# A hybrid decoder step on one Trainium2 core: a triangular product cut into two column tiles, transpositions for diagonal products, earlier cached keys, and other ranks

## The chip, the core and the metric

The kernel runs on one core of a Trainium2 chip. TensorE (PE in the profile; its weight loads are listed apart as PEld) multiplies, VectorE (DVE), ScalarE (ACT) and GpSimd (POOL) work on data in SBUF and PSUM, and SyncE (SP) issues the DMAs. Each engine runs its own instructions in order and waits on semaphores for the others. The metric is the device time of one execution in microseconds; lower is better.

## The reference

One inference step of a two-layer trunk with model width 1024, for a prompt of 1024 tokens and for 8 samples of 4 tokens each. Each layer adds a gated branch to its input. Layer 0 is sliding-window attention (16 heads of 64, 4 key and value heads, window 128, one learned sink per head); the samples attend to 128 cached tokens as well. Layer 1 is gated DeltaNet (16 value heads and 8 query and key heads of 128). Cut to what matters here:

```python
def modulate(x, c, norm_g, w_mod, b_mod):
    shift, scale, gate = jnp.split(jax.nn.silu(c) @ w_mod + b_mod, 3, axis=-1)
    return rms_norm(x, norm_g) * (1 + scale[:, None]) + shift[:, None], gate[:, None]

def swa_branch(h, w_in, sinks, w_out, k_buf=None, v_buf=None):
    q, k, v, z = jnp.split(h @ w_in, ..., axis=-1)
    attn = sink_softmax(...) @ v          # over the window, and the cache for samples
    return (attn * jax.nn.silu(z)) @ w_out, new_k, new_v

def gated_delta_chunked(q, k, v, g, beta, s0, chunk):
    ...
    lower = jnp.where(strict, jnp.einsum('nbhik,nbhjk->nbhij', kb, kc) * decay, 0.0)
    rhs = jnp.concatenate([vc * bc[..., None], kb * jnp.exp(gc)[..., None]], axis=-1)
    sol = lax.linalg.triangular_solve(lower + jnp.eye(chunk), rhs, left_side=True, lower=True, unit_diagonal=True)
    ...
    s_final, o = lax.scan(step, s0, (w_v, w_k, qk, q_dec, k_dec, g_tot))

for layer in range(2):
    hp, gp = modulate(xp, c_prompt, ...)          # the same for the samples
    op, *new = swa_branch(...) if layer == 0 else gdn_branch(...)
    xp = xp + gp * op
y_prompt = rms_norm(xp, final_norm_g)
```

## The kernel before

All tensors are float32. A large product (input and output weights of both layers) is made of three float32r products per tile: each operand is split in a high and a low part (`wh`, `wl` for weights, `h2hi`, `h2lo` for activations, `whi`, `wlo` and `ohi`, `olo` for the attention's output weights and their input), and high by high, high by low and low by high are summed in PSUM. These **weight products** (`ps_pj`, and `ps_mi` for the attention's output) are most of TensorE's stream, and they are written out as one long sequence.

Everything else is written as Python generators that `weave` puts in the list `jobs`, sorted by a rank from the tables K, KT (near the end) and KR (one row for each pair of heads). After each weight product `stages()` goes through the list in this order and lets each generator run on as long as the condition that it yields is true. `ready`, `soon` and `idle` compare the time at which a tile is finished, by the estimate of a planner (`Core`), with the time that TensorE has come to; `bank` waits for a PSUM bank, `later`, `pos` and `ticks` count products. So ranks and the other number tables (SP, AT, EX, TB, SW, MS, MM) decide between which weight products a generator's instructions stand in each engine's fixed order. Nearly every instruction is issued through one helper, so its line in the profile is 84.

The places that the change touches:

- `invert`, once for each of eight pairs of heads. It inverts unit lower triangular matrices of 128 rows in blocks of 32: DVE inverts the 32x32 diagonal blocks, POOL writes them transposed and spread into the two tiles `Xd`, and `diagonal()` multiplies, for each of four tiles of four matrices (`UZ`, one tile for a `cp_`), the matrix with `Xd` on TensorE: four products of 128 rows and 128 columns of weights with 96 moving columns. ACT copies the result with its sign turned into `M` (three buffers from the pool). `blocks()` then works the off-diagonal blocks out with narrow products of `M` and `UZ`, 32 columns of weights at a time, in the trace `ps_lg<-UZ,M`.
- `shape(i, ...)`, once for each of nine row blocks of the input of layer 1. It scales the block's rows with the reciprocal root of their mean square and turns the block. Up to step five (i below 5) DVE scales the rows (`xn`) and TensorE transposes four 128x128 pieces for each of two halves; from i = 5 on DVE makes a diagonal matrix `dg` of the scales, and TensorE multiplies the unscaled rows `xt` by it, which turns and scales at once.
- `cached`, once the prompt's attention is finished. It opens a pool, fetches the samples' mask `smk`, and starts four generators `cached_pair`, of two samples each. Each fetches its cached keys `KT` and values `vc` (two buffers of each), then multiplies queries (`qz`) with the cached keys and the new ones (`kxs`).
- `load_wo`, which fetches the attention's output weights in pieces of 128x512 and splits them. Each piece is two DMAs of 64 rows, from two heads' rows.

The lines of `diagonal` that matter most:

```python
for q in range(4):
    nc.tensor.matmul(pmv[:, q, 0:96], uz[:, q, :], xd[:, q, 0:96], start=True, stop=True)
yield soon(pm)
M = gs.tile([P, 4, 96], F32, tag="M", name="M", bufs=3)
nc.scalar.activation(M, pmv[:, :, 0:96], AF.Copy, scale=-1.0)
```

Of the kernel before, what the change touches and what calls it, by code (L numbers as in the profile page):

```python
# [5 lines left out]
F32 = mybir.dt.float32  # L6
# [8 lines left out]
P = 128  # L15
# [282 lines left out]
def body(tc, I, O, cst_ap, dbg=None):  # L298
    nc = tc.nc
# [15 lines left out]

    nkeep = COFF["wmask"][0]
    ZB, VB, SB = 2, 3, 6
    SP = (5, 21)
    AM = (7, 12)
    AT = (-1, 10)  # L320
    EX = (2.2, 1.5, 0.8, 0)
    ES, EN, EL, EM = EX
    K = {'split': 52, 'add': 3, 'attend': 12, 'turning': 14, 'modulate': 16, 'cached': 29, 'wo': 6, 'turn': 0, 'ahead': 2, 'taps': 2, 'gating': 5, 'decay': 27, 'samples': 9, 'load': 6, 'mod': 9, 'shape': 3, 'decays': 33, 'prepare': 1, 'gather': 11, 'finish': 37, 'states': 27, 'core': 2, 'new': 18}
    KT = {'prepare': 0, 'gather': 35, 'finish': 60, 'states': 19, 'core': 7, 'new': 19, 'load': 27, 'gating': 6, 'samples': 7, 'output': 23}
    KR = [{'chain': 1, 'output': 3, 'solve': 5, 'invert': 21, 'blocks': 35, 'decayed': 0}, {'chain': 10, 'output': 4, 'solve': 19, 'invert': 10, 'blocks': 35, 'decayed': 37}, {'chain': 23, 'output': 2, 'solve': 17, 'invert': 19, 'blocks': 33, 'decayed': 9}, {'chain': 23, 'output': 23, 'solve': 3, 'invert': 4, 'blocks': 24, 'decayed': 17}, {'chain': 13, 'output': 3, 'solve': 12, 'invert': 10, 'blocks': 35, 'decayed': 40}, {'chain': 9, 'output': 13, 'solve': 6, 'invert': 20, 'blocks': 51, 'decayed': 28}, {'chain': 0, 'output': 1, 'solve': 16, 'invert': 20, 'blocks': 45, 'decayed': 11}, {'chain': 10, 'output': 6, 'solve': 4, 'invert': 28, 'blocks': 1, 'decayed': 44}]
    TB = (3, 1)
    SW = (1, 10)
    MS = (44, 11)
    AH, AI = (a / 10 for a in AM)
    VK = (1,)  # L330
    MM = (1, 7)
    ORDER = [("q", 2), ("q", 3), ("q", 4), ("q", 5), ("z", 0), ("k", 1), ("z", 1), ("z", 2), ("q", 6), ("q", 7),
             ("z", 3), ("z", 4), ("z", 5), ("z", 6), ("z", 7)]
    SE = ("vector", "vector", "vector", "vector")
# [240 lines left out]
    def ready(*ts):  # L575
        return lambda: plain() or nc.ready(ts) <= nc.free["tensor"]
# [433 lines left out]
    if True:  # L1010
# [271 lines left out]
        def cached():  # L1282

            nonlocal sa_guard, sa
            yield lambda: attended[0] == 4 * NB
            at_guard.__exit__(None, None, None)
            open_wo(4)
            sa_guard = tc.tile_pool(name="sa", bufs=1, side="left")
            sa = Watched(nc, sa_guard.__enter__(), since=nc.free["tensor"])
            smk = sa.tile([P, 4, P + TS], F32, name="smk")  # L1290
            o, w = COFF["smask"]
            nc.sync.dma_start(smk.rearrange("p a c -> p (a c)"), cst_ap[:, o:o + w])
            osb = yield from bank("ob")
# [21 lines left out]
        def cached_pair(b2, smk, osv):  # L1315

            vc_rows = I["cache_swa_v"][0].rearrange("b s h d -> b s (h d)")
            yield lambda: paired[0] >= b2 - 1
# [4 lines left out]
            nc.sync.dma_start(vc, vc_rows[bs].rearrange("b s c -> s b c"))  # L1323
            yield ready(KT)
            lg = yield from bank("lg")
            for c0, c1 in ((P, P + TS), (0, P)):
# [80 lines left out]
        wo_rows = I["swa_w_out"][0]  # L1407
        wo_guards, whi, wlo = [], [], []

        def open_wo(n):  # L1410
# [8 lines left out]
        def load_wo(j0):  # L1419

            pieces = [(j, hf) for j in range(j0, j0 + 4) for hf in range(2)]
            raws_ = []
            if j0:
                yield over("ahead")

            def fetch():
                if pieces:
                    j, hf = pieces.pop(0)
                    pr, g = j // 4, j % 4
# [112 lines left out]
    if True:  # L1542
# [63 lines left out]
        def shape(i, t, xt, ss, parts):  # L1606
# [6 lines left out]
            nc.vector.tensor_scalar(sv, sv, 1.0 / D, EPS, ALU.mult, ALU.add)  # L1613
            rs = sm.tile([P, 1], F32, tag="rs", name="rs")[0:parts]
            rsqrt(nc, sm, rs, sv, 1, parts)
            if i >= 5:
                dg = x2.tile([P, 512], F32, tag="xn", name="dg", bufs=2)[0:parts, 0:parts]
                nc.vector.tensor_scalar_mul(dg, ident[0:parts, 0:parts], rs)
            for kk in range(2):
                if i < 5:  # L1620
                    xn = x2.tile([P, 512], F32, tag="xn", name="xn", bufs=2)[0:parts]
                    yield idle("vector", rs, xt)
                    nc.vector.tensor_scalar_mul(xn, xt[:, kk * 512:(kk + 1) * 512], rs)
                    yield ready(xn)
                else:
                    yield ready(dg, xt)
                pt = yield from bank("lg")
                for q in range(4):
                    if i < 5:
# [102 lines left out]
    gbs = gk.tile([P, 2, HV], F32, name="gbs")  # L1732
    gbT = gk.tile([2 * HV, TS], F32, name="gbT")

    gs, Xd, gs_guard = None, [], None

    def decays():

# [138 lines left out]
    if True:  # L1877
# [205 lines left out]
        def invert(hq, st, Ld, Xdd):  # L2083
# [31 lines left out]
            def diagonal():  # L2115

                for cp_, uz in enumerate(uzs):
# [824 lines left out]
    for b in range(LB + 1):  # L2942
# [14 lines left out]


_INS = ["x_prompt", "x_sample", "cache_swa_k", "cache_swa_v", "state_gdn_s",
        "w_mod", "b_mod", "swa_sinks", "swa_w_out", "gdn_a_log",  # L2960
        "gdn_dt_bias", "gdn_o_norm_g", "gdn_w_out", "final_norm_g"]


def relaid(inputs):
# [18 lines left out]
    more = dict(keep=keep.reshape(2, P, 16, 24),  # L2983
                keysT=A["cache_swa_k"][0].reshape(4, 2, P, 4, 64).transpose(0, 4, 1, 3, 2).reshape(4, 64, 1024),
                sinks_r=np.repeat(np.stack([A["swa_sinks"][0].reshape(4, 4)] * 2, axis=1).reshape(32), 4).reshape(P, 1),
                taps=A["gdn_conv_w"].reshape(P, P).T, gwab=gw[:, :, 6144:6176],
# [35 lines left out]
```

## Time and profile before

| | before |
|---|---|
| median of 3 runs | 1624.63 us |
| the runs | 1621.93 to 1625.57 us |
| the profiled execution | 1620.58 us |
| its span, first to last instruction | 1618.8 us |
| mean granted TensorE clock | 0.994 |
| memory traffic over the span | 121 GB/s |

The profile is of one execution. An engine's busy time counts the time in which at least one of its instructions runs, and each record of a product lasts from its start to its modelled end, so successive records overlap; what a product costs is read from the distance of starts, not from the lengths. A float32 product leaves two records and a float32r product one. In a row such as `ps_lg<-Xd,UZ 128*128 128x96 f32 x8` stand what is written, what is read, the rows and columns of the array in use, the shape of the result, the type and the number of records. A row of waits names who waited for whom. The granted clock is the share of full speed that the throttle leaves TensorE.

### The profile page before, as it was taken

To read this page: it belongs to the slowest core of one execution; us is meant where nothing else is said; L and a number is where in the kernel's file an instruction comes from. 1 tells how busy PE (TensorE), PEld (TensorE's weight loads), DVE (VectorE), ACT (ScalarE), POOL (GpSimd) and SP (SyncE) were. 2 spreads that over 40 slices of the span, in tenths; PEclk is the share of its full clock that TensorE was granted. 3 is DMA by queue.
4 is the path that set the end of the run, shared out by engine and by line. 5 is a ranking of instruction groups with operands and counts; after the bars stand their busy time and mean duration, and the time that the engine had idled before them with its cause. 6 is when DMAs were issued, how large, how long until landed. Compare 5 with 4: busy or idle time off the path is not lost. (4 is left out here: it accounts for less than half of the span.)

```text
span 1618.8 us, 30542 instructions
## 1 busy us (share of the span) xinstructions
PE 1579.1 (98%) x10586; PEld 1403.9 (87%) x10586; DVE 1208.0 (75%) x3773; ACT 841.4 (52%) x2422; POOL 222.4 (14%) x292
## 2 busy tenths in 40 slices
PE   9999999999999999999999999999999999999997
PEld 6888898988778999999989999899999997757776
DVE  5737677565566778977888778887797987848676
ACT  4625555553344646466564664664657564524332
POOL 1300000002222002010020100101002004233433
PEclk9999999999999999999999999999999999999999
DMA  9443200125343333312432324224233236685874
GB/s 363 153 165 105 79 29 28 34 69 135 106 146 108 94 83 85 107 52 77 129 78 80 103 62 121 74 70 115 75 101 91 48 94 200 204 267 182 302 262 159
DMA packets 178827, 195.71 MB, mean 121 GB/s; under 512 B 76848, under 2 KB 120720, under 8 KB 178640
## 3 DMA queue, kind: packets, MB, share of 16 engines
q1 hardware_dynamic: 178672, 193.75, 39.7%
q8 instruction: 84, 1.38, 0.4%
q14 instruction: 71, 0.58, 0.1%
HBM read 146.45 MB, written 49.27 MB: 121 GB/s over the span
## 5 line engine op out<-in xcount | busy, mean ns | idle before, releaser
L84 PE MATMUL ps_pj<-h2hi,wl 128*128 128x384 f32 (+1 forms) x1128 | 379.7, 337 | 2.4 <-DVE wl L84 2.4
L84 PE MATMUL ps_pj<-h2lo,wh 128*128 128x384 f32 (+1 forms) x1128 | 378.1, 335 | 0.0
L84 PE MATMUL ps_pj<-h2hi,wh 128*128 128x384 f32 (+1 forms) x1128 | 378.0, 335 | 0.0
L84 PEld LDWEIGHTS ps_pj<-h2hi,wl 128*128 128x128 f32 x1128 | 212.6, 188 | 6.3 <-DVE wl L84 3.4
L84 PEld LDWEIGHTS ps_pj<-h2hi,wh 128*128 128x128 f32 x1128 | 212.7, 189 | 3.1 <-ACT XR L84 0.5
L84 PEld LDWEIGHTS ps_pj<-h2lo,wh 128*128 128x128 f32 x1128 | 212.8, 189 | 2.6
L84 PE MATMUL ps_pj<-hlo,wh 128*128 128x384 f32 (+1 forms) x376 | 125.1, 336 | 0.1
L84 PE MATMUL ps_pj<-hhi,wh 128*128 128x384 f32 (+1 forms) x376 | 124.2, 332 | 0.7 <-ACT hhi L84 0.4
L84 PE MATMUL ps_pj<-hhi,wl 128*128 128x384 f32 (+1 forms) x376 | 123.5, 332 | 0.0
L84 POOL TENSOR_TENSOR Xd<-Xc,cst 32x128 f32<-32x128 f32 x128 | 66.1, 516 | 414.7 <-DMA Xc<-Xdd 97.5
L84 DVE SCALAR_TENSOR_TENSOR vT<-XR,cT,vT 128x384 f32<-128x384 f32 (+1 forms) x144 | 81.4, 575 | 26.1 <-ACT vT L84 24.7
L84 DVE TENSOR_TENSOR wl<-wr,wh 128x512 fp32r<-128x512 f32 x120 | 82.5, 688 | 11.2 <-ACT wh L84 10.6
L84 POOL TENSOR_TENSOR xt<-xt,y 128x512 f32<-128x512 f32 (+1 forms) x47 | 64.4, 1373 | 164.6 <-DVE y L84 146.6
L84 ACT CAST wh<-wr 128x512 fp32r<-128x512 f32 x128 | 78.5, 615 | 14.3 <-PE ps_pj L84 11.8
L84 PEld LDWEIGHTS ps_pj<-hlo,wh 128*128 128x128 f32 x376 | 71.3, 190 | 11.8 <-issue 10.9
L84 PEld LDWEIGHTS ps_pj<-hhi,wh 128*128 128x128 f32 x376 | 71.3, 190 | 5.4 <-issue 2.7
L84 PEld LDWEIGHTS ps_pj<-hhi,wl 128*128 128x128 f32 x376 | 71.4, 190 | 4.8 <-issue 4.6
L84 ACT ACTIVATE qe<-ps_mi,Eg 128x128 f32<-128x128 f32 x112 | 35.0, 363 | 74.3 <-PE ps_mi L84 74.2
L84 ACT COPY XR<-ps_pj 128x384 f32<-128x384 f32 (+1 forms) x96 | 43.3, 452 | 52.5 <-PE ps_pj L84 52.2
L84 ACT ACTIVATE prob<-prob,nm 128x256 f32<-128x256 f32 (+1 forms) x128 | 62.4, 490 | 15.6 <-DVE nm L84 15.5
L84 DVE TENSOR_TENSOR X<-X,tmp 128x126 f32<-128x126 f32 (+22 forms) x248 | 63.7, 257 | 8.5
L84 DVE TENSOR_TENSOR tmp<-X 128x126 f32<-128x126 f32 (+22 forms) x248 | 62.3, 251 | 7.5 <-POOL X L84 3.2
(557 smaller groups left out, 3861.1 us busy)
## 6 DMA issues: line engine op xcount, KB each, us to landing
wr<-in_gwb SPq DMA_DIRECT2D x96, 256.0 KB
S<-in_states SPq DMA_DIRECT2D x42, 256.0 KB
wm<-in_wm SPq DMA_DIRECT2D x16, 512.0 KB
wr<-in_winb SPq DMA_DIRECT2D x32, 256.0 KB
wmod<-in_w_mod SPq DMA_DIRECT2D x32, 256.0 KB
wm<-in_w_mod SPq DMA_DIRECT2D x32, 256.0 KB
DP<-gcr SPq DMA_DIRECT2D x64, 128.0 KB
zl<-zd SPq DMA_DIRECT2D x32, 256.0 KB
```

What stands on the lines that cost most here:

```text
L84: inst = fn(*args, **kwargs)
```

## The change

The product with `Xd` is cut in two for each matrix, by columns of weights: columns 64 to 127 with 96 moving columns, and columns 32 to 63 with 32. Columns 0 to 31 are no longer computed, and of columns 32 to 63 only the first 32 results. The copy to `M` becomes two operations, and the three buffers of `M` are tiles of their own whose rows 0 to 63 are set to zero once, on POOL.

`shape` scales and transposes in all nine steps (the threshold becomes DG = 9, so `dg` is not made). The cached keys and values of the first two pairs of samples are fetched as soon as the pool is open, ahead of the mask. The host lays the attention's output weights out by pieces (`wob`), and each piece is one DMA of 128 rows. The number tables are others.

```diff
-    SP = (5, 21)
+    SP = (1, 18)
-    AT = (-1, 10)
-    EX = (2.2, 1.5, 0.8, 0)
+    AT = (-1, 13)
+    EX = (1.7, 0.7, 1.0, 0)
-    K = {'split': 52, ... 'modulate': 16, ... 'gather': 11, 'finish': 37, 'states': 27, 'core': 2, 'new': 18}
+    K = {'split': 7, ... 'modulate': 22, ... 'gather': 14, 'finish': 1, 'states': 32, 'core': 0, 'new': 13}
...
-    TB = (3, 1)
-    SW = (1, 10)
-    MS = (44, 11)
+    TB = (3, 0)
+    SW = (2, 24)
+    MS = (60, 4)
-    MM = (1, 7)
+    DG = 9
+    MM = (6, 9)
...
+            held = [cached_rows(b2) for b2 in range(2)]
             smk = sa.tile([P, 4, P + TS], F32, name="smk")
...
-                weave(cached_pair(b2, smk, osv), "cached")
+                weave(cached_pair(b2, smk, osv, held), "cached")
...
+        def cached_pair(b2, smk, osv, held):
+            yield lambda: paired[0] >= b2 - 1
+            KT, vc = held[b2] if b2 < 2 else cached_rows(b2)
             yield ready(KT)
...
-                    for a in range(2):
-                        hd = (2 * pr + a) * 4 + g
-                        nc.sync.dma_start(raw[64 * a:64 * a + 64], wo_rows[hd * 64:hd * 64 + 64, hf * 512:(hf + 1) * 512])
+                    nc.sync.dma_start(raw, I["wob"][j, hf])
...
-            if i >= 5:
+            if i >= DG:
                 dg = x2.tile([P, 512], F32, tag="xn", name="dg", bufs=2)[0:parts, 0:parts]
...
-                if i < 5:
+                if i < DG:
                     xn = x2.tile([P, 512], F32, tag="xn", name="xn", bufs=2)[0:parts]
...
+        for i in range(3):
+            Mx.append(gs.tile([P, 4, 96], F32, name=f"M{i}"))
+            nc.gpsimd.memset(Mx[i][0:64], 0.0)
...
                     for q in range(4):
-                        nc.tensor.matmul(pmv[:, q, 0:96], uz[:, q, :], xd[:, q, 0:96], start=True, stop=True)
+                        for r0, n in ((64, 96), (32, 32)):
+                            rs = slice(r0, 2 * r0)
+                            nc.tensor.matmul(pmv[rs, q, 0:n], uz[:, q, rs], xd[:, q, 0:n], start=True, stop=True,
+                                             skip_group_check=True)
                     yield soon(pm)
-                    M = gs.tile([P, 4, 96], F32, tag="M", name="M", bufs=3)
-                    nc.scalar.activation(M, pmv[:, :, 0:96], AF.Copy, scale=-1.0)
+                    M = Mx[(4 * hq + cp_) % 3]
+                    nc.scalar.activation(M[64:P], pmv[64:P, :, 0:96], AF.Copy, scale=-1.0)
+                    nc.scalar.activation(M[32:64, :, 0:32], pmv[32:64, :, 0:32], AF.Copy, scale=-1.0)
```

In TensorE's order, the first block of products with `Xd` in the program stands like this before; a row gives the line, the operation, what is written and read, and the rows and columns of the result (with the number of products, where several alike follow each other):

```order
L84 MATMUL ps_pj<-h2hi,wl 128x384
L84 MATMUL ps_pj<-h2hi,wh 128x288
L84 MATMUL ps_pj<-h2lo,wh 128x288
L84 MATMUL ps_lg<-Xd_6467,UZ 128x96 x4
L84 MATMUL ps_pj<-h2hi,wl 128x288
```

And like this after, at the same block, between weight products of another width:

```order
L84 MATMUL ps_lg<-erl,qT 128x128 x4
L84 MATMUL ps_pj<-h2hi,wl 128x384
L84 MATMUL ps_lg<-Xd_6488,UZ 64x96
L84 MATMUL ps_lg<-Xd_6488,UZ 32x32
L84 MATMUL ps_lg<-Xd_6488,UZ 64x96
L84 MATMUL ps_lg<-Xd_6488,UZ 32x32
L84 MATMUL ps_lg<-Xd_6488,UZ 64x96
L84 MATMUL ps_lg<-Xd_6488,UZ 32x32
L84 MATMUL ps_lg<-Xd_6488,UZ 64x96
L84 MATMUL ps_lg<-Xd_6488,UZ 32x32
L84 MATMUL ps_pj<-h2hi,wh 128x384
```

Four products in a row have become eight, and the part of the array changes between each and the next. The block stands 111 rows later in the list; what surrounds it is the same kind of weight product.

On SP, at the place where the prompt's attention is finished and `cached` begins, before (`wr` and `wor` are pieces of the attention's output weights, `smk` is the mask, `KT` and `vc` the cached keys and values):

```order
L84 DMA wr<-in_swa_w_out 64x512 x2
L84 DMA smk<-in_cst 128x640
L84 DMA wor<-in_swa_w_out 64x512 x6
L84 DMA KT<-in_keysT 64x1024
L84 DMA vc<-in_cache_swa_v 128x2x256
L84 DMA KT<-in_keysT 64x1024
L84 DMA vc<-in_cache_swa_v 128x2x256
L84 DMA wor<-in_swa_w_out 64x512 x10
```

And after:

```order
L84 DMA wr<-in_wob 128x512 x3
L84 DMA KT<-in_keysT 64x1024
L84 DMA vc<-in_cache_swa_v 128x2x256
L84 DMA KT<-in_keysT 64x1024
L84 DMA vc<-in_cache_swa_v 128x2x256
L84 DMA smk<-in_cst 128x640
L84 DMA wor<-in_wob 128x512 x4
L84 DMA KT<-in_keysT 64x1024
```

The keys have moved ahead of the mask and of the first pieces of weights. On TensorE, 42 weight products stand between the last attention product of the prompt and the first product with keys of the samples before, and 17 after.

On TensorE again, at the first half of step six of `shape`, before (`dg` by the rows `xt`):

```order
L84 MATMUL ps_mi<-whi,ohi 128x512
L84 MATMUL ps_mi<-whi,olo 128x512
L84 MATMUL ps_lg<-dg,xt 128x128 x4
L84 MATMUL ps_mi<-wlo,ohi 128x512
L84 MATMUL ps_mi<-whi,ohi 128x512
```

And after (`xn` are the scaled rows, `erl` the tile with the identity matrix):

```order
L84 MATMUL ps_mi<-whi,olo 128x512
L84 MATMUL ps_mi<-wlo,ohi 128x512
L84 MATMUL ps_lg<-erl,xn 128x128 x4
L84 MATMUL ps_mi<-whi,ohi 128x512
L84 MATMUL ps_mi<-whi,olo 128x512
```

Four products with a diagonal have become four transpositions, and they stand behind a weight product of another part (`wlo,ohi`).

More of the change, by code (lines that the diff above doesn't have):

```diff
@@ L317, in body @@
     ZB, VB, SB = 2, 3, 6
-    SP = (5, 21)
+    SP = (1, 18)
     AM = (7, 12)
-    AT = (-1, 10)
-    EX = (2.2, 1.5, 0.8, 0)
+    AT = (-1, 13)
+    EX = (1.7, 0.7, 1.0, 0)
     ES, EN, EL, EM = EX
-    K = {'split': 52, 'add': 3, 'attend': 12, 'turning': 14, 'modulate': 16, 'cached': 29, 'wo': 6, 'turn': 0, 'ahead': 2, 'taps': 2, 'gating': 5, 'decay': 27, 'samples': 9, 'load': 6, 'mod': 9, 'shape': 3, 'decays': 33, 'prepare': 1, 'gather': 11, 'finish': 37, 'states': 27, 'core': 2, 'new': 18}
@@ L324, in body @@
-    KT = {'prepare': 0, 'gather': 35, 'finish': 60, 'states': 19, 'core': 7, 'new': 19, 'load': 27, 'gating': 6, 'samples': 7, 'output': 23}
-    KR = [{'chain': 1, 'output': 3, 'solve': 5, 'invert': 21, 'blocks': 35, 'decayed': 0}, {'chain': 10, 'output': 4, 'solve': 19, 'invert': 10, 'blocks': 35, 'decayed': 37}, {'chain': 23, 'output': 2, 'solve': 17, 'invert': 19, 'blocks': 33, 'decayed': 9}, {'chain': 23, 'output': 23, 'solve': 3, 'invert': 4, 'blocks': 24, 'decayed': 17}, {'chain': 13, 'output': 3, 'solve': 12, 'invert': 10, 'blocks': 35, 'decayed': 40}, {'chain': 9, 'output': 13, 'solve': 6, 'invert': 20, 'blocks': 51, 'decayed': 28}, {'chain': 0, 'output': 1, 'solve': 16, 'invert': 20, 'blocks': 45, 'decayed': 11}, {'chain': 10, 'output': 6, 'solve': 4, 'invert': 28, 'blocks': 1, 'decayed': 44}]
@@ L326, in body @@
-    TB = (3, 1)
-    SW = (1, 10)
-    MS = (44, 11)
+    K = {'split': 7, 'add': 3, 'attend': 12, 'turning': 14, 'modulate': 22, 'cached': 29, 'wo': 6, 'turn': 0, 'ahead': 2, 'taps': 2, 'gating': 5, 'decay': 27, 'samples': 9, 'load': 6, 'mod': 9, 'shape': 3, 'decays': 33, 'prepare': 1, 'gather': 14, 'finish': 1, 'states': 32, 'core': 0, 'new': 13}
+    KT = {'prepare': 0, 'gather': 15, 'finish': 33, 'states': 19, 'core': 7, 'new': 20, 'load': 37, 'gating': 6, 'samples': 7, 'output': 23}
+    KR = [{'chain': 1, 'output': 3, 'solve': 18, 'invert': 21, 'blocks': 35, 'decayed': 0}, {'chain': 8, 'output': 4, 'solve': 14, 'invert': 10, 'blocks': 35, 'decayed': 37}, {'chain': 23, 'output': 5, 'solve': 17, 'invert': 22, 'blocks': 23, 'decayed': 9}, {'chain': 23, 'output': 23, 'solve': 3, 'invert': 4, 'blocks': 24, 'decayed': 17}, {'chain': 27, 'output': 3, 'solve': 16, 'invert': 10, 'blocks': 35, 'decayed': 38}, {'chain': 9, 'output': 13, 'solve': 6, 'invert': 20, 'blocks': 47, 'decayed': 28}, {'chain': 0, 'output': 1, 'solve': 17, 'invert': 21, 'blocks': 45, 'decayed': 11}, {'chain': 10, 'output': 6, 'solve': 4, 'invert': 12, 'blocks': 1, 'decayed': 44}]
@@ L1313, in body, with cached_rows @@
         paired, looked = [0], [0]
-        def cached_pair(b2, smk, osv):
+        def cached_rows(b2):
             vc_rows = I["cache_swa_v"][0].rearrange("b s h d -> b s (h d)")
-            yield lambda: paired[0] >= b2 - 1
             bs = slice(2 * b2, 2 * b2 + 2)
@@ L1628, in shape @@
                 for q in range(4):
-                    if i < 5:
+                    if i < DG:
                         nc.tensor.transpose(pt[:, q * parts:(q + 1) * parts], xn[:, q * P:(q + 1) * P],
@@ L1733, in body @@
     gbT = gk.tile([2 * HV, TS], F32, name="gbT")
-    gs, Xd, gs_guard = None, [], None
+    gs, Xd, Mx, gs_guard = None, [], [], None
     def decays():
@@ L2959 @@
 _INS = ["x_prompt", "x_sample", "cache_swa_k", "cache_swa_v", "state_gdn_s",
-        "w_mod", "b_mod", "swa_sinks", "swa_w_out", "gdn_a_log",
+        "w_mod", "b_mod", "swa_sinks", "gdn_a_log",
         "gdn_dt_bias", "gdn_o_norm_g", "gdn_w_out", "final_norm_g"]
@@ L2982, in relaid @@
     gw = A["gdn_w_in"][0].reshape(KD, P, -1).transpose(1, 0, 2)
-    more = dict(keep=keep.reshape(2, P, 16, 24),
+    wo = np.asarray(inputs["swa_w_out"])[0].reshape(2, 2, 4, 64, 2, 512).transpose(0, 2, 4, 1, 3, 5)
+    more = dict(wob=wo.reshape(8, 2, P, 512), keep=keep.reshape(2, P, 16, 24),
                 keysT=A["cache_swa_k"][0].reshape(4, 2, P, 4, 64).transpose(0, 4, 1, 3, 2).reshape(4, 64, 1024),
```

3 lines of the change are left out of this document (1 added, 2 removed).

## The prediction

> **What bounds the kernel now.** First the page's header and its busy shares, then the waits of PE, then the timeline of PE around the places that the change touches.
>
> ```profile
> span 1618.8 us, 30542 instructions
> ```
>
> ```profile
> PE 1579.1 (98%) x10586; PEld 1403.9 (87%) x10586; DVE 1208.0 (75%) x3773; ACT 841.4 (52%) x2422; POOL 222.4 (14%) x292
> ```
>
> PE is busy for 98% of the span; the next engine, DVE, for 75%. So 39.7 us are left in which PE is idle, the start and the end of the program among them. Its waits (us in total, times, the longest):
>
> ```profile
> PE ps_mi L84 <- DVE us L84: 4.1, 4, 2.0
> ```
>
> ```profile
> PE ps_lg L84 <- DVE xn L84: 0.2, 1, 0.2
> ```
>
> These are the largest of 26 rows, 30 us together, and one of the smallest (one wait for a scaled block, of which more below), spread from the start to the last output blocks. Nothing waits long. What the kernel takes is therefore the length of PE's own stream: a product that takes longer there lengthens the run by as much, and an operation on another engine costs nothing until PE waits for it. The profiled execution took 1620.58 us, 1.8 more than its span; the three runs have their median 4.1 above it, at 1624.63, and all three lie 1.3 to 5.0 above it.
>
> **Xd's products, the term that decides.** Each of the 32 blocks (eight pairs of heads, four tiles each) has four products on PE, each of which leaves two records, and before they stand between weight products. First a place with a smaller block, for the step between two weight products, then a block of Xd (the columns are start, length to the end of the last, engine, what; 128*128 is rows and columns of the array in use):
>
> ```profile
> 636.68 0.34 PE L84 MATMUL ps_pj<-h2hi,wh 128*128 128x384 f32 x1
> 636.86 0.34 PE L84 MATMUL ps_pj<-h2lo,wh 128*128 128x384 f32 x1
> 637.13 0.44 PE L84 MATMUL ps_lg<-UZ,M 128*32 128x32 f32 x8
> 637.50 0.44 PE L84 MATMUL ps_pj<-h2hi,wl 128*128 128x384 f32 x1
> 637.78 0.34 PE L84 MATMUL ps_pj<-h2hi,wh 128*128 128x384 f32 x1
> ```
>
> ```profile
> 635.09 0.34 PE L84 MATMUL ps_pj<-h2hi,wl 128*128 128x384 f32 x1
> 635.27 1.03 PE L84 MATMUL ps_lg<-Xd,UZ 128*128 128x96 f32 x8
> 636.08 0.42 PE L84 MATMUL ps_pj<-h2hi,wh 128*128 128x384 f32 x1
> 636.34 0.34 PE L84 MATMUL ps_pj<-h2lo,wh 128*128 128x384 f32 x1
> ```
>
> From one weight product to the next is a step of 0.18 (636.68 to 636.86). In the second fence 1.25 us pass from the weight product before the block to the second one after it; without the block they would be two such steps, rather 0.17 than 0.18. The block costs **0.91 us**: eight records of 0.11, and nothing for going in and out.
>
> After, each product becomes two, one into columns 64 to 127 of the array with 96 moving columns and one into columns 32 to 63 with 32. The trace of before has no such pair, but it has narrow products, 128*32, of both widths of movement, 32 columns at 637.13 above and 96 here:
>
> ```profile
> 848.75 0.34 PE L84 MATMUL ps_pj<-h2lo,wh 128*128 128x384 f32 x1
> 849.02 0.85 PE L84 MATMUL ps_lg<-UZ,M 128*32 128x96 f32 x8
> 849.80 0.44 PE L84 MATMUL ps_pj<-h2hi,wl 128*128 128x384 f32 x1
> 850.08 0.34 PE L84 MATMUL ps_pj<-h2hi,wh 128*128 128x384 f32 x1
> ```
>
> By the same reckoning the block of 96 costs 1.33 - 0.34 = 0.99 and that of 32 costs 0.92 - 0.34 = 0.58. The 64 columns between them cost 0.41 over eight records, 0.05 each; in proportion a record of 96 columns is 0.077 and one of 32 is 0.026. That leaves 0.37 in both blocks for going into a narrow part of the array and out again. So a narrow block is no gain by itself even if its two halves run side by side: 0.99 for 0.91.
>
> The question is what it costs to go from a 64-column part to a 32-column part and back, which the new stream does seven times within each block. There is one place before where the two follow each other between products of one size:
>
> ```profile
> 414.29 0.39 PE L84 MATMUL ps_pj<-wlo,ohi 128*64 128x512 f32 x1
> 414.52 0.40 PE L84 MATMUL ps_pj<-whi,ohi 128*64 128x512 f32 x1
> 414.85 1.05 PE L84 MATMUL ps_lg<-modG,sels 128*32 128x512 f32 x2
> 415.83 0.45 PE L84 MATMUL ps_pj<-wlo,ohi 128*64 128x512 f32 x1
> ```
>
> Between two of 128*64 the step is 0.23; to the first of 128*32 it is 0.33, 0.10 more. On the way back two records of 512 columns, 0.41 each at the rate above, fill 0.98: 0.16 more. The weights tell the same:
>
> ```profile
> 414.85 0.14 PEld L84 LDWEIGHTS ps_lg<-modG,sels 128*32 128x32 f32 x2 [0.42 <-issue]
> ```
>
> They are loaded only when their product starts, after 0.42 of idle, and no engine is named that they waited for. And it isn't shared columns that hold them: here the part changes from columns 64 to 127 to columns 0 to 31,
>
> ```profile
> 378.66 0.41 PE L84 MATMUL ps_ob<-spT,vc 128*64 128x16 f32 x6
> 379.00 0.33 PE L84 MATMUL ps_lg<-kxs,qz 64*32 64x32 f32 x16
> ```
>
> and 0.34 pass for six records of 16 columns, which at the 0.03 to 0.04 that they take one after another are 0.2; some 0.13 is left over. So I take it that each change of size empties the array. Then nothing runs side by side: 8 x 0.077 + 8 x 0.026 + 0.37 + seven changes. At 0.10 each the block is 1.89, at 0.16 it is 2.31. If each change cost half of the 0.37, it were 2.49; if none cost anything, and the halves overlapped, 0.99. I take 0.14 between the two directions of the nearest row, 2.17, less the 0.37 where a block follows another narrow one (8 of the 32 by the order of the instructions, so 0.1 on average): 2.07, **1.16 more than before, 37 us for 32 blocks**. The ends are +31 and +51 with emptying, and +2.6 without it.
>
> The Trainium skill has rules for both, in "TensorEngine Tiling (Array Packing)", Tiling Modes, Key Properties: a change of tiling mode, not just of tile, drains TensorE, and it lists 128 x 64 and 128 x 32 as different modes. By that rule the sum is the one with emptying, and the 0.10 at 414.85 agrees with it; no trace of before shows the two sizes side by side on different columns with all 128 rows.
>
> **Steps turned by transposition (DG 5 to 9).** Four blocks, steps six to nine, lose eight groups of four products with a diagonal and get eight groups of four transpositions:
>
> ```profile
> 478.41 0.39 PE L84 MATMUL ps_mi<-whi,olo 128*128 128x512 f32 x1
> 478.64 1.05 PE L84 MATMUL ps_lg<-dg,xt 128*128 128x128 f32 x8
> 479.45 0.48 PE L84 MATMUL ps_mi<-wlo,ohi 128*128 128x512 f32 x1
> 479.76 0.40 PE L84 MATMUL ps_mi<-whi,ohi 128*128 128x512 f32 x1
> ```
>
> ```profile
> 452.96 0.39 PE L84 MATMUL ps_mi<-whi,ohi 128*128 128x512 f32 x1
> 453.19 0.60 PE L84 MATMUL ps_lg<-erl,xn 128*128 128x128 f32 x4
> 453.55 0.48 PE L84 MATMUL ps_mi<-whi,olo 128*128 128x512 f32 x1
> 453.86 0.39 PE L84 MATMUL ps_mi<-wlo,ohi 128*128 128x512 f32 x1
> ```
>
> Less two steps of 0.23, 0.89 becomes 0.44: **-3.6 us**. DVE scales two halves of a row block in place of one diagonal; the earlier steps do that now, and PE waited for xn once, for 0.2, so I take 0; if each of the eight new ones cost as much it were 1.6.
>
> **Cached keys first.** Before, the mask and six half rows of weights stand ahead of the keys on SP's queue, and PE waits:
>
> ```profile
> 354.21 0.33 SPq L84 DMA_DIRECT2D smk<-in_cst  x1
> 354.60 4.53 SPq L84 DMA_DIRECT2D wor<-in_swa_w_out  x6
> 359.18 0.59 SPq L84 DMA_DIRECT2D KT<-in_keysT  x1
> ```
>
> ```profile
> 363.43 0.64 PE L84 MATMUL ps_lg<-KT,qz 64*32 64x128 f32 x16 [2.48 <-DMA vc<-in_cache_swa_v]
> ```
>
> ```profile
> 364.00:368.00 4.00, 4.00 (x45) 3.14 (x42) 1.30 (x8) 0.62 (x1) 0.00 (x0) 0.56 1.06 254
> 368.00:372.00 4.00, 4.00 (x16) 4.00 (x15) 2.28 (x4) 3.04 (x10) 2.32 (x2) 0.59 0.60 143
> ```
>
> The third number from the end of such a window's row is the granted clock: 0.56 and 0.59 of full speed right behind the wait, 1.8 + 1.6 = 3.4 us lost. The wait costs 5.9 in all. After, the keys go out 4.97 earlier against the pool's opening (354.21 in place of 359.18) and took at most 4.3 to land; the order puts their first product 17 weight products behind the last attention block in place of 42, 25 x 0.17 = 4.3 us sooner. So the keys gain about 0.7 us on PE, and more, since 256 KB of keys no longer share the engines with a mask and six loads ahead of them. I take **-4**; the ends are 0 (they still come late) and -5.9. Whole rows of weights halve SP's issues for them; no row of the waits names wor, so 0.
>
> **The eviction in two.** ACT's copy of the product becomes two:
>
> ```profile
> L84 ACT ACTIVATE M<-ps_lg 128x384 f32<-128x384 f32 x32 | 15.7, 489 | 33.2 <-PE ps_lg L84 33.2
> ```
>
> The first of them reads as many columns as that row's, the second a third, so 0.49 is the most that the second can take: 32 x 0.49 = 16 us of ACT, which is 52% busy. What waits for M comes up to 0.49 later in each block; PE has weight products of 0.17 ready in between, three of them, so I take 0 of it; with that cover gone it were 16. Clearing three M tiles on POOL (14% busy) happens once: 0.
>
> **The other ranks and numbers.** They move products on PE among the weight products; neither the count nor the kinds change. What they can give is a part of the 30 us of waits, what they can take are new ones of the same sizes; I take 0 and 8 us either way.
>
> **Sum.** 1620.6 + 37 - 3.6 - 4 = 1650.0. The runs stand 1.3 to 5.0 above the profiled execution; I leave the forecast at **1650**, its own range being 1638 to 1664.
>
> **Rivals.** The first one leans on a place where three narrow tiles stand together:
>
> ```profile
> 840.71 0.85 PE L84 MATMUL ps_lg<-UZ,M 128*32 128x96 f32 x24
> ```
>
> *The halves run side by side.* If a change between parts with different columns empties nothing, a block is 0.99: 2.6 - 3.6 - 4 = -5.0, or 1615.6, and with up to 8 us from the ranks 1609 to 1622. This ends on the other side. For it speaks that 128*32 parts of different columns do run so (24 records in this row last 0.85, as long as the 8 at 849.02); it decides if a change costs under 0.02, since 7 x 32 x 0.02 = 4.5 uses up the gain. Against it stand the three rows above. The Trainium skill says in the same place that different tiles can load weights and multiply in parallel; by that sentence the time would be this rival's. Chance 0.31, of which 0.26 faster and 0.05 within 0.2%. *Emptying at a lower price.* Where only part of the 0.10 is paid (0.04 a change), a block is 1.35 to 1.45: 32 x 0.5 = 16, so 1629. Chance 0.08, slower. *New waits.* The scaled halves, the second eviction or the new order make PE wait 8 to 12 us more, beside either case: 1624 to 1628 with the halves side by side. Chance 0.05, of which 0.02 slower and 0.03 within 0.2%. The forecast has the other 0.56.
>
> Over 0.2%, 3.2 us, is about what a measurement of this kernel can tell from no change. So slower 0.56 + 0.08 + 0.02 = 0.66, within 0.2% 0.05 + 0.03 = 0.08, faster 0.26. Cases of both signs hold the chance, so the range goes from 1610, which takes in most of the first rival, to 1663.
>
> **What would show it.** In the profile after, the four products of a block follow each other at 0.4 to 0.5 us a pair, with their weight loads not ahead of them; PE's busy time rises while its instructions gain only 224 records. A pair every 0.16 shows the rival. The wait for the keys and the clock behind it in the slice at 360 us are gone or not; transpositions of 0.44 stand in steps six to nine. Wrong would the forecast be by the price of a change of size, before all else.

## The result, and the profile after

The changed kernel takes **1663.13 us** (median of 4 runs, 1661.94 to 1664.1) against 1623.28 us before in the same comparison (4 runs): ratio 1.0245, 95% interval 1.0227 to 1.0263. It is slower, as forecast, but by 40 us in place of 25, and it lies just above the range that ended at 1663 (the forecast's own range, before the rivals were joined to it, went to 1664).

The header and the busy shares of the profile after:

```profile
span 1660.2 us, 31020 instructions
PE 1617.9 (97%) x10810; PEld 1410.7 (85%) x10810; DVE 1206.5 (73%) x3777; ACT 854.6 (51%) x2454; POOL 219.6 (13%) x295
```

The span is 41.4 us longer. PE is busy for 38.8 us more with 224 records more (10586 to 10810), and idle for 2.6 us more. So most of the time went into TensorE's stream itself. The timeline of TensorE around the first block with `Xd` (start, length to the end of the last, what) shows where:

```profile
638.09 0.42 PE L84 MATMUL ps_pj<-h2hi,wl 128*128 128x384 f32 x1
638.44 2.02 PE L84 MATMUL ps_lg<-Xd,UZ 128*64 128x96 f32 x16
640.39 0.44 PE L84 MATMUL ps_pj<-h2hi,wh 128*128 128x384 f32 x1
640.66 0.34 PE L84 MATMUL ps_pj<-h2lo,wh 128*128 128x384 f32 x1
```

By the prediction's reckoning the block is 2.57 - 0.35 = 2.22 us (the group's name shows the first of its two forms). Before it was 0.91. The weight loads don't run ahead of the products, as the prediction said of emptying; the first starts only when its product does:

```profile
638.43 1.91 PEld L84 LDWEIGHTS ps_lg<-Xd,UZ 128*64 128x64 f32 x16 [0.18 <-issue]
```

Of the other two terms the profile after shows both effects where they were looked for. The keys land nearly in time, and the clock behind them is full (third number from the end of the window's row):

```profile
363.87 0.64 PE L84 MATMUL ps_lg<-KT,qz 64*32 64x128 f32 x16 [0.57 <-DMA KT<-in_keysT]
```

```profile
364.00:368.00 4.00, 4.00 (x63) 3.35 (x59) 0.74 (x5) 0.19 (x1) 0.00 (x0) 1.00 1.03 334
```

And all nine steps are transposed, with hardly a wait. The row has the eight steps of 128 rows (records, busy time and mean, and the idle time ahead of them); the ninth, of 32 rows, has 8 records of its own:

```profile
L84 PE MATMUL ps_lg<-erl,xn 128*128 128x128 f32 x64 | 9.7, 273 | 0.7 <-DVE xn L84 0.7
```

What was not expected are the first three rows of TensorE's waits:

```profile
PE ps_mi L84 <- DVE us L84: 7.4, 7, 1.6
PE ps_mi L84 <- DVE S L84: 5.4, 7, 1.9
PE ps_mi L84 <- ACT kb L84: 4.8, 5, 1.6
```

They were 4.1, 0.5 and 0.6 before. `us` and `S` belong to the recurrence of layer 1, `kb` to the samples' state updates near the end. They take the place of the keys' wait and of others that are gone.

### The profile page after: what moved, and what is told of

It reads as the page before. It is cut to its first block, busy times and chain, and to the rows that moved or that the text cites. A ratio compares the mean times of both kernels' runs of the same rounds, so it can differ in the third digit from the quotient of the medians.

```text
span 1660.2 us, 31020 instructions
## 1 busy us (share of the span) xinstructions
PE 1617.9 (97%) x10810; PEld 1410.7 (85%) x10810; DVE 1206.5 (73%) x3777; ACT 854.6 (51%) x2454; POOL 219.6 (13%) x295
## 5 line engine op out<-in xcount | busy, mean ns | idle before, releaser
L84 ACT CAST wh<-wr 128x512 fp32r<-128x512 f32 x128 | 78.3, 614 | 28.7 <-PE ps_pj L84 27.6
L84 ACT COPY XR<-ps_pj 128x384 f32<-128x384 f32 (+1 forms) x96 | 43.3, 451 | 45.3 <-PE ps_pj L84 44.7
L84 PE MATMUL ps_lg<-Xd,UZ 128*64 128x96 f32 (+1 forms) x512 | 64.6, 239 | 0.2 <-POOL Xd L84 0.2
```

Of the source, the lines that this page charges most:

```text
L84: inst = fn(*args, **kwargs)
```

## The experiments

**A measure used below.** Where two traces differ in many places, the time from the start of each of TensorE's records to the start of the next is compared with the usual step of its kind (the 30th percentile, over the traces of all kernels here, of steps with the same part of the array, the same width and the same kind of neighbours). The sum of the usual steps is what the stream costs undisturbed; the rest is **delay**, by waits and by a lower clock. Both are worked out from single profiled executions, and over the first 1200 weight products, where nothing is changed but a number or two, kernels differ by up to 1.4 us in it. Against the kernel before, over the whole program:

| kernel | undisturbed stream | delay |
|---|---|---|
| changed kernel | +31.6 | +9.8 |
| before, split products, order kept (o_before_split) | +35.2 | +1.7 |
| changed kernel, whole products, order kept (o_whole) | -3.6 | +16.5 |
| before, DG = 9, order kept (o_dg) | -3.5 | +6.8 |
| before, keys first and whole rows, order kept (o_keys_wob) | 0.0 | +1.7 |

The measure does not serve where two products run side by side, as with even tiles (below): there the starts of two streams lie between each other, 0.01 and 0.08 us apart in turn, and a usual step means little. Where the order is kept, the 32 blocks can be compared directly, from the weight product before a block to the second one after it. Read so, they take 35.5 us more in o_before_split and 0.4 more in o_before_even than in the kernel before, and 36.0 less in o_whole, 35.8 less in o_even and 24.1 less in o_grouped than in the changed kernel.

### One edit undone or done, planned anew

```diff
# e1_xd_only: the kernel before with
+ for r0, n in ((64, 96), (32, 32)): matmul(pmv[rs, q, 0:n], uz[:, q, rs], xd[:, q, 0:n])   # and M in two
# e2_no_xd: the changed kernel with
+ matmul(pmv[:, q, 0:96], uz[:, q, :], xd[:, q, 0:96])                                      # and M in one
# e3_even: the changed kernel with
+ for rs, n in ((slice(64, P), 96), (slice(0, 64), 32)):
# e4_grouped: the changed kernel with the loop over tiles outside the loop over q
```

> The kernel before with one edit, the product with Xd in two column tiles (64 and 32 columns) and M in two evictions; ranks, numbers, DG and DMAs are those of before. If each change of size empties the array, a block costs 2.2 us in place of 0.90 and the kernel takes 32 x 1.2 to 1.3, that is 38 to 42 us more than before: ratio 1.023 to 1.026. If the other ranks and numbers of the changed kernel are what lengthened it, this edit alone gives less than 15 us: ratio under 1.009.

Measured 1682.14 us, ratio 1.0366 (1.0351 to 1.0382): more than the whole change, and more than either theory gave.

> The changed kernel with the product with Xd whole again (128 columns, one eviction of M); ranks, DG = 9, early keys and whole rows of weights stay. If the size changes are the cause, 38 to 42 us go: 1621 to 1625, ratio to before 0.998 to 1.001, and what is left of the difference is what the rest of the change does. If the ranks are the cause it stays above 1645, ratio over 1.013.

Measured 1654.77 us, ratio 1.0201 (1.0182 to 1.0219). Taken alone this would speak for the ranks and against the price of the size changes.

> The changed kernel with the second tile made as wide as the first: columns 0 to 63 with 32 moving columns in place of columns 32 to 63 (the results for columns 0 to 31 are not used). As many products, on different columns, but all of one size. If changes of size are paid, none is left inside a block: 16 records take about 8 x 0.08 and what of 8 x 0.05 does not lie beside them, with 0.37 for entry and exit, so 1.0 to 1.4 a block, 27 to 39 us less than the changed kernel: 1624 to 1636, ratio to before 1.000 to 1.008. If eight narrow products are dear by themselves, whatever their sizes, it stays at 1655 to 1665, ratio over 1.019.

Measured 1640.34 us, ratio 1.0109 (1.0092 to 1.0125).

> The changed kernel with the four products of 64 columns first and then the four of 32: the same products, one change of size inside a block in place of seven. At 0.14 a change a block is 0.84 less: 27 us off the changed kernel, 1636, ratio to before 1.006 to 1.010. If the products are dear by themselves it stays at 1655 to 1665.

Measured 1645.26 us, ratio 1.0128 (1.0101 to 1.0154).

These four don't add up: 58 us for the split put into the one kernel, 8 us for taking it out of the other. The edits are not alone in these runs, because of the planner. It holds an estimate for each product, and a block of other products shifts all later estimates, so that every condition after the first block fires at another place. Each of the four is a new order, and their delay shows it: +29.0 for e1_xd_only and +43.3 for e2_no_xd, worked out as above. So the edits had to be made without moving anything.

### One edit undone or done, with every instruction in its place

In the following kernels the planner is told of the instructions that it had planned, while others are issued:

```diff
+ def swap(self, real, planned):
+     kept = ...                              # the planner's estimates
+     for eng, op, args, kwargs in real: getattr(getattr(self, eng), op)(*args, **kwargs)
+     ...                                     # estimates put back
+     for eng, op, args, kwargs in planned: self.issued(eng, op, None, args, kwargs)
...
+ nc.swap(whole, split)      # o_whole; o_even and o_grouped alike, in the changed kernel
+ nc.swap(split, whole)      # o_before_split, in the kernel before
+ nc.swap(even, whole)       # o_before_even, in the kernel before
```

> The changed kernel with every instruction where it stands, but each block's eight split products replaced by the four whole ones (both evictions of M stay). The planner is fed the split products, so nothing else is moved. If the size changes are the cost, a block falls from 2.2 to 0.90 and 32 x 1.3 = 42 us go: 1621, ratio to before 0.997 to 1.000. If the order that the new ranks make is slow by itself, PE's idle time stays up and the kernel takes 1630 to 1650, as the re-planned run with whole products (1654.8) did.

Measured 1633.49 us, ratio 1.0058 (1.0039 to 1.0077). 29.6 of the 39.9 us go with the split, and 10 us stay, which the order and the smaller edits hold.

> The changed kernel with every instruction where it stands, the second tile of each pair widened to columns 0 to 63, so that all eight products of a block have one size. If only changes of size cost, and products of one size on different columns run side by side, a block is 1.0 to 1.2 and the kernel 3 to 10 us above the same order with whole products: 1624 to 1631. If they don't lie side by side, 1.4 a block and 1637. If narrow products are dear whatever their sizes, 1655 to 1665.

Measured 1631.77 us, ratio 1.0049 (1.0032 to 1.0066): no more than whole products in the same order. Eight products in two tiles on different columns cost hardly anything extra as long as the tiles have one size (0.10 us a block by the traces).

> The changed kernel with every instruction where it stands, but in each block the four products of 64 columns first and then the four of 32: one change of size inside a block in place of seven. At 0.14 a change 6 x 0.14 x 32 = 27 us go: 1636. If the products themselves are dear, 1655 to 1665.

Measured 1638.54 us, ratio 1.0089 (1.006 to 1.0119): 25 us less than the changed kernel, with the very same products in another sequence. Its block in the timeline of TensorE:

```profile
637.74 0.42 PE L84 MATMUL ps_pj<-h2hi,wl 128*128 128x384 f32 x1
638.09 1.24 PE L84 MATMUL ps_lg<-Xd,UZ 128*64 128x96 f32 x16
639.26 0.44 PE L84 MATMUL ps_pj<-h2hi,wh 128*128 128x384 f32 x1
639.54 0.34 PE L84 MATMUL ps_pj<-h2lo,wh 128*128 128x384 f32 x1
```

That is 1.80 - 0.35 = 1.45 us, 0.77 less than the 2.22 above, for six changes of size fewer: **0.13 us a change**. In the trace of the changed kernel a record starts 0.18 us behind the last one of 64 columns when the size changes, and 0.13 behind the last one of 32; here, between records of one size, it is 0.08 and 0.03. The rule of the Trainium skill, "TensorEngine Tiling (Array Packing)", Tiling Modes, Key Properties, by which a change of mode drains TensorE, agrees with this; the price is from these runs.

> The kernel before with every instruction where it stands, only the products with Xd split in two tiles of two sizes and M evicted in two. If the size changes are the cost: 32 x 1.3 = 42 us more, 1666, ratio 1.024 to 1.027; the 58 us more of the re-planned run (1682.1) then hold 16 us of new waits that a new order made. If the split costs as much without a new order, 1680.

Measured 1655.66 us, ratio 1.0191 (1.0167 to 1.0214): 32 us for the split, 1.0 us a block. Its profile and that of before differ by 36.9 us of span. A block by itself costs 1.25 more in this order; where it stands beside other narrow products it is 1.05, since there it shares the way in and out with them.

The last run of this kind came at the end, to see whether even tiles make a kernel faster than both:

> The kernel before with every instruction where it stands, the products with Xd in two tiles of one size (columns 64 to 127 with 96 moving columns, columns 0 to 63 with 32; results for columns 0 to 31 not used) and M evicted in two. If products of one size on different columns run side by side, a block of 16 records takes no longer than the 8 whole ones: 1619 to 1624, ratio 0.997 to 1.000. If only the change of size were dear in the split and the halves didn't overlap, 32 x 0.3 to 0.5 = 10 to 16 us more: ratio 1.006 to 1.010.

Measured 1625.52 us, ratio 1.0014 (1.0003 to 1.0025): no gain. A block in its timeline takes 1.00 us (1.35 - 0.35), just what the prediction's rival of halves side by side gave, 0.99:

```profile
635.64 0.34 PE L84 MATMUL ps_pj<-h2hi,wl 128*128 128x384 f32 x1
635.91 0.88 PE L84 MATMUL ps_lg<-Xd,UZ 128*64 128x96 f32 x16
636.71 0.44 PE L84 MATMUL ps_pj<-h2hi,wh 128*128 128x384 f32 x1
636.99 0.34 PE L84 MATMUL ps_pj<-h2lo,wh 128*128 128x384 f32 x1
```

Over all 32 blocks that is 0.4 us more than before: a block by itself is 0.10 dearer, one beside other narrow products 0.09 cheaper. So there was nothing to gain.

### The small terms, alone, in the order of before

```diff
# o_dg
+ nc.swap([scale both halves], [scale the diagonal])
+ nc.swap([four transpositions], [four products with dg])
# o_keys_wob
+ held = [cached_rows(b2) for b2 in range(2)]     # ahead of smk on SyncE
+ nc.swap([one DMA of 128 rows], [two DMAs of 64 rows])
# o_best: both
# o_wob: the second line of o_keys_wob alone
```

> The kernel before with every instruction where it stands, but steps six to nine scale both halves of a row block and transpose them, in place of the diagonal. If the prediction's term is right, 8 x (0.89 - 0.44) = 3.6 us go: 1620, ratio 0.997 to 0.999. If the second scaling on VectorE makes TensorE wait, nothing is gained: ratio 0.999 to 1.002.

Measured 1625.07 us, ratio 1.0017 (1.0007 to 1.0027): no gain. The stream is 3.5 us shorter, as predicted, but delay is up by 6.8. Some 3.8 of it come between the weight products 1500 and 2100, where the new scalings stand. VectorE takes 0.88 us for the two scalings of a block (0.29 for the diagonal before), and TensorE now waits for VectorE's `olo`, and once where the profile names no engine:

```profile
500.56 0.50 PE L84 MATMUL ps_mi<-whi,olo 128*128 128x512 f32 x1 [0.38 <-DVE olo L84]
519.76 0.36 PE L84 MATMUL ps_lg<-h2hi,wab 128*64 128x384 f32 x1 [0.71 <-issue]
```

Against before, 0.65 and 0.87 us are lost at these two places, and the same two losses stand in o_best below, which has the same edit. Another 1.5 go with a lower clock that comes later, while TensorE is busy throughout; it is not in o_best at this place, so it isn't shown to be the edit's:

```profile
520.00:535.00 15.00, 15.00 (x98) 13.46 (x96) 7.82 (x15) 7.89 (x15) 0.00 (x0) 1.00 0.07 19
535.00:540.00 5.00, 5.00 (x23) 4.92 (x23) 2.89 (x8) 1.95 (x3) 0.00 (x0) 0.66 0.01 2
```

> The kernel before with every instruction of the engines where it stands; on SyncE's queue the first two pairs' keys and values go ahead of the mask, and a piece of the attention's output weights is one DMA of 128 rows. TensorE's first product with keys stays where it is, so the keys have 5 us more: the wait of 2.5 us goes, and with it the 3.4 us of lower clock behind it. 1618, ratio 0.995 to 0.998. If the weights that now come later make TensorE wait instead, or the lower clock has another cause, 1621 to 1624, ratio above 0.998.

Measured 1623.91 us, ratio 1.0005 (0.9994 to 1.0015): the second case. The wait for the keys is gone, and this one stands 5 us further on (PE's timeline, then DVE's):

```profile
368.31 0.66 PE L84 MATMUL ps_pj<-hhi,wh 128*128 128x384 f32 x1 [3.15 <-DVE zss L84]
```

```profile
365.57 0.69 DVE L84 TENSOR_TENSOR wlo<-wor,whi 128x512 fp32r<-128x512 f32 x1 [7.09 <-ACT whi L84]
```

The weights `wor` now land behind keys and mask; ACT splits them first thing, DVE waits 7.09 us for ACT's part, and behind DVE's instruction in its queue stands the work that frees PE's bank. In the changed kernel the planner knew of the new sequence and moved that work, and there the gain is seen at first: after 1500 weight products its delay stands 6.3 us below that of before. Most of it doesn't last. After 1800 weight products it is about 1 us below, and between them TensorE waits 0.65 for `whi` and 0.54 for `wlo`, parts of the weights that now stand behind the keys.

> Both of the former together in the order of the kernel before, with the whole products with Xd. If the two terms add up, 7 to 9 us less than before: 1615, ratio 0.994 to 0.996, faster than both kernels.

Measured 1623.74 us, ratio 1.0005 (0.9996 to 1.0014): no faster than before.

> The kernel before with every instruction where it stands, only the pieces of the attention's output weights as one DMA of 128 rows each in place of two of 64. Three issues then stand between the mask and the keys in place of six, so the keys go out some 2 us earlier without any weights behind them coming later: the wait of 2.5 us shrinks to under 1 and the lower clock behind it may go. 1618 to 1621, ratio 0.996 to 0.999, faster than both kernels. If one DMA of 128 rows takes as long to issue as two, nothing changes: 0.999 to 1.001.

Measured 1624.43 us, ratio 1.0 (0.9991 to 1.0008). The keys did go out 3 us earlier (359.18 before, SyncE's row here), and their first product started no earlier (363.43 before):

```profile
356.15 0.55 SPq L84 DMA_DIRECT2D KT<-in_keysT  x1
```

```profile
363.79 0.64 PE L84 MATMUL ps_lg<-KT,qz 64*32 64x128 f32 x16 [2.69 <-DMA KT<-in_keysT]
```

As many bytes as before stand ahead of the keys, in half as many issues, which fits a queue that is held up by bytes. This is not shown, though: the next weights, behind the keys, went out earlier as well (358.94 where it was 361.60) and may have shared the way with them.

### The numbers

Left over are the 10 us of o_whole, whose stream is 3.6 us shorter and whose delay is 16.5 us up. In the changed kernel three of the recurrence's steps stand back to back, with no weight product in between; these are the second and the third, and the window around them, after and then before:

```profile
704.13 0.70 PE L84 MATMUL ps_mi<-us,ktok 128*128 128x256 f32 x2 [1.51 <-DVE us L84]
708.85 0.70 PE L84 MATMUL ps_mi<-us,ktok 128*128 128x256 f32 x2 [0.70 <-DVE us L84]
```

```profile
698.00:710.00 12.00, 8.91 (x51) 6.78 (x50) 10.09 (x34) 6.70 (x21) 0.00 (x0) 1.00 0.59 156
```

```profile
698.00:710.00 12.00, 12.00 (x130) 10.48 (x126) 9.49 (x24) 4.05 (x10) 1.35 (x3) 1.00 0.08 25
```

PE is busy 8.91 of 12 us, where it was busy throughout. In the order of the kernel before no two steps stand together: its first recurrence begins 2589 weight products into the program and must end at the 2840th; in the changed kernel it begins at the 2704th and must end at the same place. Four kernels take closing numbers, numbers and DG back, with whole products:

```diff
# o_whole_close: o_whole with AT, EX, KT, SW, TB of before
# w_dg5: o_whole with DG = 5
# w_numbers: o_whole with SP, K, KR, MS, MM of before
# w_numbers_dg5: both
```

> The run with the changed kernel's order and whole products (1633.5), but the numbers that act only after the last head's projections (AT, EX, KT, SW, TB) are those of before; all before that stage stands where it stood. The new waits for kb, 7.5 us, lie in that stage and those on us and S mostly ahead of it. If the closing numbers cost as much as their waits, 1624 to 1628; if what the new order costs lies ahead of it, 1631 to 1637.

Measured 1645.34 us, ratio 1.014 (1.0126 to 1.0154): 12 us slower with the closing numbers of before. The changed ones fit this order better.

> The kernel of the run with whole products (1633.5: the changed kernel's numbers, early keys and whole rows, no split), with the diagonal products in steps six to nine again, planned anew. The recurrence starts 60 weight products after the place of before rather than 115; three of its steps still stand back to back. If DG = 9 with its later start is what costs, 1624 to 1629; if it gives the 3.6 us that the prediction took, 1637; if the stacked steps cost by themselves, no more than 3 us off: 1630 to 1634.

Measured 1654.2 us, ratio 1.0182 (1.0168 to 1.0196).

> The kernel of the run with whole products (1633.5) with SP, K, KR, MS and MM of the kernel before and DG = 9, planned anew. Here seven steps of the first recurrence stand back to back in place of three. If stacked steps cost, some 1.5 us each as at 704 and 709 us, 6 us more: 1637 to 1644. If the changed numbers are what costs, they are gone here: 1622 to 1628.

Measured 1652.45 us, ratio 1.0166 (1.0147 to 1.0186). The window in which most of the seven stacked steps stand:

```profile
710.00:730.00 20.00, 14.32 (x68) 11.21 (x69) 11.78 (x44) 8.74 (x33) 0.00 (x0) 0.91 0.27 79
```

> Both taken back: SP, K, KR, MS and MM of before and the diagonal products from step six, with the closing stage's numbers, early keys and whole rows of the change. The recurrence starts 12 weight products earlier than in the kernel before and no step is stacked. If late start and stacking are the cause, their 8 us and more go: 1618 to 1626. If every new plan costs by itself, 1630 to 1640.

Measured 1634.99 us, ratio 1.006 (1.0044 to 1.0075): no step is stacked, and it is no faster than o_whole.

Between the 2700th and the 3000th weight product, where the first recurrence ends, the delay rises against before by 2.9 us with no step stacked (w_numbers_dg5), by 8.8 and 8.4 with three (o_whole, w_dg5) and by 18.6 with seven (w_numbers). So stacked steps go with some 2 us of delay each. But this is one place: w_numbers_dg5 loses as much elsewhere. No single number or edit explains the 10 us, and every order that the planner made anew for these experiments, eight with o_whole_close, has 16 to 43 us more delay than the kernel before. That the numbers of each kernel fit only its own order is consistent with all of this, but not shown; which of them matter stays open.

## Why the prediction came out as it did

*Xd's products* were right in mechanism and nearly in size. That changes of size are what costs, o_even and o_grouped show, which keep the products and take the changes away. A change costs 0.13 us where 0.14 was taken, an isolated block 2.22 (2.16 in the order of before) where 2.17 was taken, and the 32 blocks 32 us by the medians in the order of before, 30 in the order of after and 35 by the undisturbed stream, against 37. That the array empties at a change fits the late weight loads; it is not seen directly.

*Transpositions* shorten the stream by 3.5 us, as the prediction said. That VectorE's part is hidden was wrong: alone, o_dg gains nothing. Of the 6.8 us of delay that came, 1.5 are lost at two waits that both kernels with this edit have; the rest isn't traced to it.

*The keys* gave what was predicted (-4) or a little more in the changed kernel, up to its 1500th weight product, and lost most of it again by the 1800th. Put alone into the order of before they only moved the wait.

*The eviction in two* was not tried by itself. o_before_even holds it, with blocks that cost 0.4 us more in all, and is 2 us above the kernel before, so the eviction costs no more than that; the bound of 16 us was far off.

*The other ranks and numbers* are the step that failed: "I take 0 and 8 us either way". The changed kernel's delay is 9.8 us above before, where the prediction had 4 below: 14 us on the wrong side, which with a stream 2 us shorter than predicted make up the 12 us between the predicted 1650.0 and the profiled execution's 1661.94. The medians say the same: without the split (o_whole) the kernel is 10 us above before, where the prediction's other terms make 7.6 below. The small terms, alone in the order of before (o_best), give nothing of the 7.6; the 10 us came with the new order, and by what mechanism stays open. The waits that the prediction read, 30 us in 26 rows, were taken as something to give and take at random, with an even chance. They may rather be what is left after the numbers were fitted to one order, so that any other order starts from more: the changed kernel and all eight orders planned anew here have more, none has less. The range should have reached upward by that much. It was luck that the result missed it by so little: the split, 5 to 7 us cheaper by the medians than forecast, hid part of the loss.

*Smaller:* the forecast was left at the profiled execution's level, though all runs lay 1.3 to 5.0 above it; the median after lies 1.2 above its own.

Time added to TensorE's stream counted in full in the profile (o_before_split: 35.5 us in the blocks, 36.9 in the span). Time taken from it came out in part: of the 36.0 us that o_whole takes out of the blocks, 28.7 are seen in the span, and some 2.8 of the missing go with a lower clock in the first 14 us and at 537 us, where the products are the same; of the 3.5 us of o_dg nothing is seen. The prediction read PE's 98% as a bound that works both ways.

## What to carry to other kernels

Where narrow products of two sizes must be done, do all of one size first, or give both one size: a change cost 0.13 us here, about as much as a small product, and tiles of one size on different columns ran side by side. Where one engine is busy 98% of the time, a small saving on it can be lost to a wait for the next engine, as with the scalings of o_dg, so look there before counting it. A new order is not free either: the eight orders planned anew here had 16 to 43 us, 1 to 2.7%, more delay than the kernel before. To price one edit in a planned kernel, keep the plan and swap the instructions; edits that are planned anew measure the plan.

## What the hardware showed beside that

A lower clock can stand right behind rather short waits of PE: 2.48 us ahead of the window at 0.56 in the kernel before, 3.15 us ahead of the 0.52 us records at 368 us in o_keys_wob (0.34 at full clock, from the same run's earlier rows). A wait is not all that matters: behind one of 1.90 us at 758 us in the changed kernel the clock is full, and in o_dg it falls to 0.66 from 535 us on though PE was busy throughout the 15 us before. Nor does the mean clock order the times of whole executions: the four of the changed kernel have 0.998, 0.993, 0.998 and 0.994 at 1661.94, 1662.68, 1663.59 and 1664.1 us.
